# In-projection as Strassen's seven products over quadrants of weights and tokens, in four blocks

## The chip, the cores and the metric

The kernel runs as one program on one core of a Trainium2 chip. The metric is the device time of one execution in microseconds (us). Where this text speaks of the engines it uses the names of the profile: PE (matrix multiply), PEld (its weight loads), DVE (vector), ACT (scalar), POOL (GpSimd) and SP (the queue from which nearly all DMAs of this kernel are issued).

## The reference, cut to what matters

One layer over 2,048 prompt tokens and 8 x 16 sample tokens, model width 1,024, everything in float32:

```
qm, km, vm, om, ip, fp, qa, ka, va = split_in(x @ w_in)   # widths 512 x4, 4, 4, 512, 128, 128
km = km * 128 ** -0.5
logi = ip + b_igate;  logf = log_sigmoid(fp + b_fgate)
hm = sigmoid(om) * head_norm(mlstm_chunkwise(qm, km, vm, logi, logf, state), g)
qa, ka = rope(qa), rope(ka)
ha = swa(qa, ka, va, sinks)                               # window of whole chunks
h = layer_norm(alpha * x + concat(hm, ha) @ w_out)
y = layer_norm(alpha * h + conv_ffn(h))
```

The change is about `x @ w_in`. Of its 2,824 columns 2,560 (qm, km, vm, om, qa) are called the five groups here; the other 264 are the gates and attention's keys and values. The result is wanted to float32 accuracy. The kernel therefore splits each operand into a high and a low part and makes every product in three matmuls (high x high, high x low, low x high).

## The kernel before

**Stages.** The 17 tiles of 128 tokens (16 is the sample tile) are worked through in blocks `BLOCKS = [[16,0,1],[2..5],[6..9],[10..13],[14,15]]`. First comes the in-projection of all five blocks (`i_block`, L379), then the out-projection with the first layer norm over the same blocks (`o_block`, L1049), then the feed-forward part in three larger blocks (`f_ups`, `f_downs`). The two feed-forward projections are already made by seven products over quadrants, the up-projection with two sets of three accumulator banks that alternate (`f_product` L1274, `f_after` L1284).

**In-projection.** Per block the query and key columns come first, feature-major: eight feature tiles, each 8 x 3 matmuls with the weights stationary and all tokens of the block (256 to 512) moving. Then `group` (L355) makes the gates-and-keys columns (264 wide) and three groups of 512 columns token-major: for each tile 8 x 3 matmuls with the tokens stationary and the weights moving. Three accumulator banks (`dps`) go round; each result is copied or rotated out of its bank (L403 to L431) through a ring of three `zev` buffers and stored to DRAM.

**Weights.** `w_split` (L298) loads a unit of 128 x 1024 weights, copies it to the high part on ACT (L194) and subtracts for the low part on DVE (L195); four raw buffers, five high and five low ones. All 24 units of a block are loaded and split again for every block. **Tokens** are loaded and split by `x_slice` (L333), eight slices per block, the low part on DVE or, from the second block on, for odd slices on POOL (L352).

**The weave.** Attention work of finished blocks (the sample chain, the mLSTM chain, the window-attention chain) is cut into steps. `Chains.weave` (L162) advances a clock by the cost that each piece of dense work yields, and puts in a chain step when it is due; a chain may use a block's results once `i_done` is past that block. `until` (L176) forces chain steps before an out-projection block loads their results. The order on PE is the order of the program; it is never changed. Five accumulator banks (`tps`) belong to the chains, so that three are left for dense work. Sums of the down-projection's weights are prepared on the way (`d_sums`, L442).

## Time and profile before

| what | value |
|---|---|
| median of 3 runs | 2448.58 us (2445.84 to 2454.03) |
| the profiled execution | 2448.26 us, its span 2446.3 us |
| granted PE clock, mean | 0.993 |
| in-projection (0 to 777 us) | PE busy 758.34, DVE 459.93, ACT 358.26, POOL 166.89, DMA share 0.63 at 205 GB/s |
| out-projection (777 to 1020 us) | PE busy 232.25, DVE 186.30, ACT 110.77, POOL 86.38, DMA share 0.61 at 209 GB/s |
| chain that ended last | PE 73%, DVE 12%, DMA 5%, issue 4%, ACT 4%, POOL 2% |

Busy time counts an instruction from start to its modelled end. A matmul's duration of 0.28 to 0.41 us in the rows includes the way through the array, which overlaps the next matmul; what a matmul costs in a stream is the distance from its start to the next one's start, which is called its pitch here. The pitch is read from the timeline, not from the mean of a group.

### The profile page before, as it was taken

To read this page: it belongs to the slowest core of one execution; us is meant where nothing else is said; L and a number is where in the kernel's file an instruction comes from. 1 tells how busy PE (TensorE), PEld (TensorE's weight loads), DVE (VectorE), ACT (ScalarE), POOL (GpSimd) and SP (SyncE) were. 2 spreads that over 40 slices of the span, in tenths; PEclk is the share of its full clock that TensorE was granted. 3 is DMA by queue.
4 is the path that set the end of the run, shared out by engine and by line. 5 is a ranking of instruction groups with operands and counts; after the bars stand their busy time and mean duration, and the time that the engine had idled before them with its cause. 6 is when DMAs were issued, how large, how long until landed. Compare 5 with 4: busy or idle time off the path is not lost.

```text
span 2446.3 us, 36879 instructions
## 1 busy us (share of the span) xinstructions
PE 2389.1 (98%) x13004; PEld 2109.5 (86%) x13004; DVE 1760.2 (72%) x3094; ACT 1205.4 (49%) x2235; POOL 398.1 (16%) x444
## 2 busy tenths in 40 slices
PE   9989999999999999999999999999999999999998
PEld 8877878778877778899999999999999978778776
DVE  5566655455477767997788776778766677896897
ACT  4324455355355533655555555445554544444543
POOL 1121322122123333300000000002000100210400
PEclk9999999999999999999999999999999999999999
DMA  8887744544557557588777889987988776656652
GB/s 276 300 302 241 232 134 139 185 126 143 178 185 244 169 208 262 181 300 305 289 267 274 266 307 321 315 283 242 327 293 263 242 275 213 233 181 217 211 189 103
DMA packets 277512, 576.14 MB, mean 236 GB/s; under 512 B 45352, under 2 KB 122156, under 8 KB 277328
## 3 DMA queue, kind: packets, MB, share of 16 engines
q1 hardware_dynamic: 275600, 567.50, 68.6%
q0 software_dynamic: 1728, 6.29, 0.7%
q8 instruction: 103, 1.69, 0.3%
q14 instruction: 81, 0.66, 0.1%
HBM read 419.92 MB, written 153.78 MB: 235 GB/s over the span
## 4 chain that ended last, share of the span: by engine, by line
PE 73%; DVE 12%; DMA 5%; issue 4%; ACT 4%; POOL 2%; SPq 0%; DVEq 0%; POOLq 0%; ACTq 0%
PE dps L1282 15%; PE fup L1282 14%; PE dps L199 8%; PE dps L200 7%; PE dps L201 7%; PE fht L1479 5%; PE dps L1479 5%; PE fup L1479 4%; DMA zf<-cc 2%; DVE cc L1330 2%; DVE wlo L195 2%; DMA ty<-wdn 1%; ACT cc L1328 1%; PE ppo L839 1%; PE ppt L833 1%
## 5 line engine op out<-in xcount | busy, mean ns | idle before, releaser
L1282 PE MATMUL dps<-hh,uw 128*128 128x384 f32 (+1 forms) x1848 | 480.5, 328 | 5.2 <-ACT u L1307 2.9
L1282 PE MATMUL fup<-hh,uw 128*128 128x384 f32 (+1 forms) x1848 | 481.1, 328 | 2.6 <-ACT u L1307 2.4
L195 DVE TENSOR_TENSOR wlo<-wraw,whi 128x1024 fp32r<-128x1024 f32 (+3 forms) x289 | 343.3, 1193 | 158.4 <-ACT whi L194 155.9
L194 ACT CAST whi<-wraw 128x1024 fp32r<-128x1024 f32 (+3 forms) x289 | 282.1, 981 | 288.6 <-PE dps L1479 94.0
L1282 PEld LDWEIGHTS dps<-hh,uw 128*128 128x128 f32 x1848 | 329.8, 188 | 7.0 <-ACT u L1307 4.1
L1282 PEld LDWEIGHTS fup<-hh,uw 128*128 128x128 f32 x1848 | 329.9, 188 | 4.9 <-ACT u L1307 3.9
L1330 DVE SCALAR_TENSOR_TENSOR cc<-u,cw,cc 128x768 f32<-128x768 f32 (+1 forms) x264 | 252.6, 978 | 109.8 <-ACT cc L1328 107.8
L199 PE MATMUL dps<-whi,xh 128*128 128x512 f32 (+1 forms) x816 | 317.7, 389 | 0.0
L200 PE MATMUL dps<-wlo,xh 128*128 128x512 f32 (+1 forms) x816 | 309.6, 379 | 2.8 <-DVE wlo L195 2.8
L201 PE MATMUL dps<-whi,xl 128*128 128x512 f32 (+1 forms) x816 | 309.6, 379 | 0.4 <-POOL xl L352 0.4
L1282 PE MATMUL fup<-hl,uw 128*128 128x384 f32 (+1 forms) x924 | 302.5, 327 | 2.4 <-DVE hl L195 2.4
L1282 PE MATMUL dps<-hl,uw 128*128 128x384 f32 (+1 forms) x924 | 302.3, 327 | 0.0
L199 PEld LDWEIGHTS dps<-whi,xh 128*128 128x128 f32 x816 | 154.9, 190 | 45.5 <-issue 16.5
L1328 ACT ACTIVATE cc<-u,cw 128x768 f32<-128x768 f32 (+1 forms) x132 | 129.6, 998 | 121.0 <-DVE u L1321 59.7
L200 PEld LDWEIGHTS dps<-wlo,xh 128*128 128x128 f32 x816 | 155.0, 190 | 31.9 <-DVE wlo L195 4.0
L201 PEld LDWEIGHTS dps<-whi,xl 128*128 128x128 f32 x816 | 154.6, 189 | 32.1 <-POOL xl L352 0.8
L1282 PEld LDWEIGHTS fup<-hl,uw 128*128 128x128 f32 x924 | 173.5, 188 | 2.8 <-DVE hl L195 2.8
L1282 PEld LDWEIGHTS dps<-hl,uw 128*128 128x128 f32 x924 | 173.5, 188 | 0.0
L1479 PE MATMUL fup<-whi,fu 128*128 128x512 f32 x484 | 158.5, 399 | 7.1 <-DVE yacc L1508 4.5
L1479 PE MATMUL dps<-whi,fu 128*128 128x512 f32 x440 | 149.0, 395 | 0.0
L1479 PE MATMUL fht<-whi,fu 128*128 128x512 f32 x396 | 132.2, 396 | 0.2 <-DVE yacc L1508 0.2
L195 DVE TENSOR_TENSOR uw<-wv,uw 128x512 fp32r<-128x512 f32 x132 | 90.7, 687 | 49.3 <-ACT uw L194 46.8
(285 smaller groups left out, 4343.0 us busy)
## 6 DMA issues: line engine op xcount, KB each, us to landing
uw<-zw SPq DMA_DIRECT2D x176, 512.0 KB, 5.1
zw<-uw SPq DMA_DIRECT2D x88, 512.0 KB, 2.9
wv<-wup SPq DMA_DIRECT2D x66, 512.0 KB, 5.2
wraw<-wtm SPq DMA_DIRECT2D x60, 512.0 KB, 4.7
wraw<-zt SPq DMA_DIRECT2D x60, 512.0 KB, 4.5
wraw<-wdn SPq DMA_DIRECT2D x45, 512.0 KB, 4.8
wraw<-wqk SPq DMA_DIRECT2D x40, 512.0 KB, 4.9
wraw<-wo SPq DMA_DIRECT2D x40, 512.0 KB, 4.7
```

The lines of the kernel that those rows point to most:

```text
L194: nc.scalar.copy(hi, src)
L195: nc.vector.tensor_sub(lo, src, hi.bitcast(F32))
L199: mm(out, ah, bh, start=start, stop=False)
L200: mm(out, ah, bl, start=False, stop=False)
L201: mm(out, al, bh, start=False, stop=stop)
L833: nc.tensor.transpose(pp[:, j * P:(j + 1) * P], scs[kvh][:, j, kt * P:(kt + 1) * P], self.ident)
L839: nc.tensor.matmul(po[64 * kvh:64 * kvh + 64], w, pts[:, kvh], start=kt == 1, stop=kt == nk)
L1282: mm(ps, l[:, k], r[:, k], start=s in (1, 7) and k == 0 and i == 0, stop=k == 3 and i == 2, skip_group_check=True)
L1328: S.activation(c[:, v], u[:, v, 2:2 + n], AF.Identity, bias=w[3], scale=w[2])
L1330: V.scalar_tensor_tensor(c[:, v], u[:, v, i:i + n], w[i], c[:, v], op0=ALU.mult, op1=ALU.add)
L1479: mm(ps, l[:, k, c], r[:, k], start=s in (1, 4, 7) and u == 0 and k == 0 and i == 0, stop=u == nu - 1 and k == n - 1 and i == 2, skip_grou ...
```

## The change

**Products.** The blocks of the in-projection become `IBLOCKS = [[0,1,2,3,16],[4..7],[8..11],[12..15]]`; the out-projection keeps its five (`OBLOCKS`). For each of the five groups of 512 columns and each block of 512 prompt tokens, weights and tokens are cut into quadrants (512 rows of the model width by 256 columns or tokens), and seven products of quadrants or of their sums take the place of eight. A product is 2 x 4 x 3 matmuls with 256 moving columns into one bank (`i_product`). The sample tile is not Strassen's: its four plain products ride on the same weights in block 0, again 256 wide. Gates, keys and values stay direct, 264 wide (`i_direct`).

**Banks.** Three banks A, B, C are held throughout (`ib`). Products 1 and 2 go to A, 6, 5 and 3 to B, 7 and 4 to C; between them ACT copies a bank out or A into B, and DVE adds C to a copy (`i_after`).

**Weight sums.** In block 0 the four quadrants of a group are loaded, and four sums are made in place on DVE and stored to DRAM (`zws`); later blocks load quadrants and sums, seven units per group. **Token sums** are made per block in place in four raw tiles (`x_steps`).

**Buffers.** Four high and four low weight buffers in place of five; weights are loaded up to four units ahead of their split. Token tiles are single, one pair for each product. In the out-projection tokens come in pairs of rows, 1024 wide (`x_pair`), and the running sums `ymix` lie in the token tiles of the in-projection. In the feed-forward part two extra weight buffers (`wx`) make up for the two taken away.

```diff
+IBLOCKS = [[0, 1, 2, 3, 16], [4, 5, 6, 7], [8, 9, 10, 11], [12, 13, 14, 15]]
+OBLOCKS = [[16, 0, 1], [2, 3, 4, 5], [6, 7, 8, 9], [10, 11, 12, 13], [14, 15]]
...
-            for b in range(nb):
-                chains.weave(self.with_sums(b, self.i_block(b)))
-                self.i_done = b + 1
+            chains.weave(self.i_dense())
...
-                if i >= 22 and n < AHEAD:
+                if n < (0, 2, 4, 5)[min(max(i - 22, 0) // 4, 3)]:
                     self.f_next()
...
+    def i_begin(self):
+        self.ib = [self.dps.tile([P, 512], F32, name="dps", tag="dps") for _ in range(3)]
...
+            if b == 0:
+                it += [("p", 0, 0, s) for s in (1, 2, 7, 6)]
+            else:
+                it += [("p", b, 0, s) for s in (1, 7, 6, 2)]
+            for g in range(NG):
+                if g:
+                    it += [("p", b, g, s) for s in (6, 2)]
+                it.append(("p", b, g, 5))
+                if g + 1 < NG:
+                    it += [("p", b, g + 1, 1), ("p", b, g, 4), ("p", b, g, 3), ("p", b, g + 1, 7)]
+                else:
+                    it += [("p", b, g, 3), ("p", b, g, 4)]
+            it += [("t", b, i, b) for i in ((2, 3, 4, 0, 1) if b == 0 else (0, 1))]
+            if b + 1 < nb:
+                it += [("t", b + 1, i, b) for i in (2, 3)]
...
+    def raw_free(self):
+        n = 3 if self.spare else 4
+        return len(self.raws) < n or all(e[1] for e in self.raws[-4:len(self.raws) - n + 1])
+
+    def advance(self):
+        while self.next_split() or self.next_raw():
+            pass
...
+    def split_first(self, g, s, hi, lo):
...
+        if s == 7:
+            V.tensor_sub(r[a11], r[a11], r[a21])
+            keep(a11, 7)
+        elif s == 6:
+            V.tensor_add(r[a21], r[a21], r[a22])
+            keep(a21, 5)
+            V.tensor_sub(r[a11], r[a22], r[a11])
+            keep(a11, 6)
...
+            self.split(hi[:, c], lo[:, c], f[:, c])
+        if s == (6 if g == 0 else 2):
+            V.tensor_sub(r[a12], r[a12], r[a11])
+            keep(a12, 3)
...
+    def i_product(self, b, g, s):
+        mm = self.nc.tensor.matmul
+        ps = self.ib[{1: 0, 2: 0, 6: 1, 5: 1, 3: 1, 7: 2, 4: 2}[s]]
+        wh, wl = self.wu["p", b, g, s]
+        hh, hl = self.hx[b, s]
+        for c in range(2):
+            m = slice(c * P, c * P + P)
+            o = ps[:, c * HT:(c + 1) * HT]
+            for k in range(4):
+                for i, (w, x) in enumerate(((wh, hh), (wh, hl), (wl, hh))):
+                    l, r = (w[:, k, m], x[:, k]) if g < 2 else (x[:, k, m], w[:, k])
+                    mm(o, l, r, start=s in (1, 7) and c == k == i == 0, stop=k == 3 and i == 2, skip_group_check=True)
+                if k % 2:
+                    yield 645
...
+    def i_after(self, b, g, s):
...
+        if s == 1 and g == 0:
+            nc.scalar.copy(B, A)
+        elif s == 6:
+            self.u2 = self.mp.tile([P, 512], F32, name="u2", tag="u2", bufs=1)
+            copy(self.u2, B)
+        elif s == 2:
+            self.i_out(b, g, 0, 0, A)
+        elif s == 5:
+            u4 = self.zev()
+            copy(u4, B)
+            add(u4)
+            self.i_out(b, g, 1, 1, u4)
+        elif s == 4:
+            add(self.u2)
+            self.i_out(b, g, 1, 0, self.u2)
+            if b == 0:
+                self.i_batch(g)
+        elif s == 3:
+            self.i_out(b, g, 0, 1, B)
+            if g + 1 < NG:
+                nc.scalar.copy(B, A)
...
+    def x_pair(self, b, p):
...
+        nc.scalar.copy(h, raw)
+        (nc.gpsimd if b < nb - 1 and p % 2 else nc.vector).tensor_sub(l, raw, h.bitcast(F32))
...
     def f_slot(self, dt=F32R):
-        self.slot = (self.slot + 1) % 2
-        return self.wp.tile([P, KD, P], dt, name="uw", tag=("whi", "wlo")[self.slot], bufs=5)
+        self.slot = (self.slot + 1) % 10
+        if self.slot < 8:
+            return self.wp.tile([P, KD, P], dt, name="uw", tag=("whi", "wlo")[self.slot % 2], bufs=WB)
+        return self.wx.tile([P, KD, P], dt, name="uw", tag="wex", bufs=2)
```

In `i_dense` the items run in this order; after each product its two weight halves are released, `i_after` is emitted, and `advance` emits the next split (for the product four places on) and the next load. `add` is on DVE: C plus the copy (scaled for the key half). `i_out` copies or rotates a finished quadrant into a `zev` buffer and stores it. The token steps run on ACT for the high part and on DVE for the low part, but on POOL for b12 and 4 in block 0 and for 2, 4 and 5 in the other blocks.

## The prediction

> **What bounds the kernel now.** I read the page's engine shares first, then the busy time by stage, then the timelines of PE and DVE.

> ```profile
> span 2446.3 us, 36879 instructions
> PE 2389.1 (98%) x13004; PEld 2109.5 (86%) x13004; DVE 1760.2 (72%) x3094; ACT 1205.4 (49%) x2235; POOL 398.1 (16%) x444
> ```

> By stage (columns: window, length, busy us of PE, PEld, DVE, ACT, POOL with instruction counts, granted clock, DMA share, GB/s):

> ```profile
> 0.00:61.00 61.00, 56.95 (x314) 53.33 (x315) 31.70 (x59) 27.42 (x47) 7.76 (x15) 1.00 0.81 276
> 150.00:777.00 627.00, 615.88 (x3572) 503.93 (x3571) 370.68 (x1160) 302.17 (x795) 139.51 (x142) 0.99 0.58 186
> 777.00:1020.00 243.00, 232.25 (x1087) 183.37 (x1086) 186.30 (x322) 110.77 (x199) 86.38 (x55) 0.97 0.61 209
> 1020.00:1900.00 880.00, 871.40 (x5237) 866.79 (x5236) 675.26 (x900) 480.07 (x815) 72.83 (x156) 1.00 0.83 287
> ```

> The reader is to see that PE is the bound in every stage, with DVE at 59% in the in-projection (370.68 of 627) and 77% behind it (186.30 of 243; 675.26 of 880). So matmul time taken out of the in-projection comes off the end, unless PE begins to wait for DVE or ACT. The pitch of a matmul is read from start to start:

> ```profile
> 676.26 0.28 PE L200 MATMUL dps<-xl,whi 128*128 128x256 f32 x1
> 676.38 0.28 PE L201 MATMUL dps<-xh,wlo 128*128 128x256 f32 x1
> 676.50 0.28 PE L199 MATMUL dps<-xh,whi 128*128 128x256 f32 x1
> 676.62 0.28 PE L200 MATMUL dps<-xl,whi 128*128 128x256 f32 x1
> ...
> 476.92 0.40 PE L200 MATMUL dps<-wlo,xh 128*128 128x512 f32 x1
> 477.15 0.39 PE L201 MATMUL dps<-whi,xl 128*128 128x512 f32 x1
> 477.38 0.40 PE L199 MATMUL dps<-whi,xh 128*128 128x512 f32 x1
> ```

> With 256 columns moving it is 0.12 (median of the last block 0.118), with 512 it is 0.2335, with 384 and 264 0.174 and 0.121. So 256 columns cost half of 512, although each has a weight load of its own; the nearest thing to a floor is the 128-column transposes, 0.11 apart (eight from 203.59 to 204.35). The new shape stands just above it.

> **The matmuls.** Before: queries and keys 192 at 0.174, 576 at 0.2335, 192 at 0.118; three groups 17 x 24 x 3 = 1224 at 0.2335; gates and keys 408 at 0.121: 33.4 + 134.5 + 22.7 + 285.8 + 49.5 = 525.9 us. After: 20 group-blocks x 7 products x 24 = 3360, and 240 for the sample tile, at 0.118 = 424.8; gates and keys unchanged 49.5; eight transposes 0.9: 475.2. **Minus 50.7 us**, all on the bounding engine.

> **What DVE and ACT get.** Rows of the first 777 us:

> ```profile
> L195 DVE TENSOR_TENSOR wlo<-wraw,whi 128x1024 fp32r<-128x1024 f32 x103 | 127.7, 1246 | 64.6 <-ACT whi L194 64.0
> L468 DVE TENSOR_TENSOR zev<-dps,ropet 128x512 f32<-128x512 f32 x17 | 11.6, 684 | 22.2 <-PE dps L201 22.2
> L352 DVE TENSOR_TENSOR xl<-xraw,xh 128x512 fp32r<-128x512 f32 x12 | 10.0, 835 | 3.3 <-ACT xh L351 3.3
> ```

> Splits of weights: 140 against 100 full units, 40 x 1.246 = 49.8, and four gate units fewer at 0.70, -2.8. Low parts of tokens on DVE: 21 x 1.246 = 26.2 against 16.5. Sums of tokens 16 and of weights 20, each 1024 wide at 1.22 (the median of L195): 43.9. Sample tile 4 x 0.69 = 2.8. The 40 additions of C, 512 wide, 40 x 0.69 = 27.6. Together +131: DVE goes from 459.9 of 777 us (59%) to 591 of about 750 (79%). ACT gets 40 splits and the larger token copies at 1.05 us and about 40 copies of 512 at 0.59: 358 + 76 = 434, 58%. DMA: 105 + 20 weight loads and 20 stores of 0.52 MB against 100 loads are +23 MB on 159, about 240 GB/s; the stage behind runs at 287 with PE busy 99%, so bandwidth costs nothing. SP's own queue: a load of weights now waits for the split four units on; as loads lie eight products (23 us) ahead and land in about 5, the cover is 15 us.

> **The start, +10 us (5 to 17).** Now the first product needs one 0.2 MB token slice and a weight unit: it starts at 6.1 us, and the first 61 us lose 8. After, nine transfers of 0.52 MB come first; the first weights land at 4.3, the later ones about 1.9 apart at 276 GB/s: the second token quadrant at 12, the fourth at 18, the last weights at 20. Product 1 can start at 8.5. Product 7 needs, from 18 on, two token sums, a weight sum and two low parts in a row on DVE (6.2 us): it starts at 24, when PE has been free since 19.5. Product 6 has 3.7 us of weight sums and splits and as much for tokens behind that: 31. By 34 PE has done 14 us of work, 20 lost, 10 more than now.

> **The banks, +13 us (0 to 45).** This is the real question. Before, a bank was filled in 5.6 us and two others were free. After, the order is 5, 1', 4, 3, 7', 6', 2': what reads a bank has the length of *one* product, 24 x 0.118 = 2.83 us, plus the chain steps put in (223 us of chain slots beside 526 dense: on average 1.2 more). Five hand-overs per group have this slack: three copies on ACT, the addition after 4 on DVE, and after 5 a copy on ACT and then an addition on DVE before 4 may write C. What they will take I read off the evictions of now, from the last matmul of the bank to the end of its reader. In the three middle blocks the 48 plain ACT copies take 0.93 in the median, 3 of them over 2.83. The 12 rotations (two DVE operations, 1.36 of service) take 1.39, 3 over 2.83. The 12 key tiles, which go ACT, DVE, ACT, take 3.2, 10 over 2.83. Where DVE is fuller (75% from 650 on) the last block's rotation is an example; its matmul was issued at 770.64 and ends at 771.04:

> ```profile
> 771.86 0.68 DVE L468 TENSOR_TENSOR zev<-dps,ropet 128x512 f32<-128x512 f32 x1
> ...
> 775.68 0.42 DVE L813 CUSTOM_DVE_ANT_0 sc<-psc,k_mswa 128x256 f32<-128x256 f32 x1
> ...
> 776.02 0.69 DVE L468 TENSOR_TENSOR zev<-dps,ropet 128x512 f32<-128x512 f32 x1
> 776.70 0.69 DVE L469 TENSOR_TENSOR rb<-dps,ropet 128x512 f32<-128x512 f32 x1
> ```

> A burst of attention on DVE stood in front, and 6.3 us went by. PE would then stand, and behind it the chains' own matmuls in the same queue. Against 4.0 us of slack I charge 0.4 us for the hand-over after 5, 0.2 after 4, 0.1 for each copy, 0.9 per group; 15 groups with chains give 13, block 0's five, without chains, nearly none. Ends: nothing, as the 80% DVE of 870 to 1020 us costs PE 1.5 us; 3 us per group, 45, if responses are like the last block's.

> **Further.** At the three block boundaries the first token pair can be overwritten only after the last direct tile; a copy of 1.05 and a low part of 1.25 then fit in the 5.8 us of two direct tiles, but the chains start at the same moment: +4 (0 to 10). In the out-projection one weight buffer fewer leaves 4.2 us between a unit's release and its next use for 2.3 us of splitting, and POOL's low parts double in width, from 1.59 to an estimated 3.2: +3 (0 to 12). [...] The chains begin later, as block 0 is longer, but by the weave's own costs the last chain tile still ends before the fourth out-projection block, as now, and no forced step arises: 0. The feed-forward start makes five instead of six weights ahead, from four steps later, each on time for products 2.1 us apart: 0 (-2 to 2).

> **Sum.** 2446.3 - 50.7 + 10 + 13 + 4 + 3 = 2425.6 span; 2.0 lie around it; **2428 us**. The profiled execution, 2448.26, is the median of the runs within 0.4, so nothing is added.

> **Rivals.**
> (1) *The slack suffices.* The hand-overs are ordered ahead of the other work and cost nothing, the start 5: 2446.3 - 50.7 + 5 + 3 + 2 = 2406. For it: 45 of 48 ACT copies inside 2.83. Against: DVE at 79%.
> (2) *Given back.* Hand-overs of 2.2 us per group (33) eat the gain: within 0.3% of now.
> (3) *Slower, by the single set of banks.* If the hand-over after 5 waits behind attention's bursts as at 771, 4 us per group, 15 x 4 = 60: 2446.3 - 50.7 + 17 + 60 + 2 = 2475. It decides from 2.7 us per group (41 us) on. For it: the 3.2 us of the ACT-DVE-ACT tiles and the up-projection, which has two sets of banks. Against: with PE standing, DVE catches up, so the wait limits itself.
> (4) *The change doesn't shorten PE.* At a pitch of 0.130 instead of 0.118 for 3600 matmuls, +43: 2471. Against: the rows above.

> **Chances.** Forecast (2410 to 2441) 0.46, (1) 0.18, (2) 0.13, (3) 0.20, (4) 0.03. Under 0.3% (7.3 us) this kernel's measurement tells no change. Faster 0.64, same 0.13, slower 0.23. The range takes in most of (1) and (3): 2402 to 2472; the forecast alone would have 2410 to 2441.

> **What would show it.** Right: the 256-wide matmuls 0.118 apart; PE waits that name copies of a bank on ACT and additions on DVE, some 13 us in all; DVE near 79% before the out-projection; first product after 8 us; feed-forward part unchanged in length. Wrong: waits on those two over 40 us, or waits for weight splits or landings; a dense stretch with a wider pitch; an out-projection or feed-forward part longer by more than 10 us.

## The result, and the profile after

The changed kernel takes 2524.38 us (median of 4 runs, 2520.63 to 2530.84) against 2447.47 us (4 runs, 2445.84 to 2454.03): 1.0312 times as long, interval 1.0282 to 1.0342. The forecast was 2428 us, so its sign was wrong, and its range, which ended at 2472, did not reach the time. The profile below is of the slowest of the four, 2530.84 us, so it shows some 6 us more than the median.

The page of the changed kernel (the span; PE's busy time; the granted PE clock in 40 slices of 63 us):

```profile
span 2529.0 us, 39907 instructions
...
PE 2372.6 (94%) x14425; PEld 2169.9 (86%) x14425; DVE 1899.0 (75%) x3181; ACT 1271.5 (50%) x2282; POOL 425.6 (17%) x431
...
PEclk9989898997998999999999999999999999999999
```

PE is busy for 16 us less than before, 2372.6 against 2389.1, and the span is 83 us longer: PE waits. The slices with a granted clock under 0.9 all lie among the first 14, ahead of the feed-forward part. By stage (columns: window, length, busy us and counts of PE, PEld, DVE, ACT, POOL, granted clock, DMA share, GB/s), the start, the in-projection from 150 us on, the out-projection and the first 880 us of the feed-forward part, which answer to the four rows of before:

```profile
0.00:61.00 61.00, 47.41 (x346) 44.92 (x347) 48.66 (x59) 29.55 (x42) 9.34 (x8) 0.94 0.80 282
150.00:799.00 649.00, 577.02 (x4444) 533.01 (x4443) 463.08 (x1153) 338.58 (x784) 174.98 (x141) 0.93 0.67 210
799.00:1096.00 297.00, 260.99 (x1280) 205.35 (x1280) 213.10 (x451) 129.68 (x254) 98.06 (x61) 0.94 0.58 189
1096.00:1976.00 880.00, 867.27 (x5192) 860.31 (x5191) 672.65 (x894) 476.85 (x807) 67.89 (x153) 1.00 0.83 286
```

The in-projection ends at 799 us instead of 777, the out-projection at 1096 instead of 1019. No engine is full in either: DVE, which the prediction feared, stands at 71% (463.08 of 649). The loss is not spread over the in-projection. The same columns for the passages from block 1 to 2 and from block 2 to 3, and for the stretch behind the second:

```profile
372.00:420.00 48.00, 32.49 (x222) 30.84 (x222) 41.24 (x107) 22.58 (x63) 26.61 (x21) 0.79 0.56 168
575.00:640.00 65.00, 43.02 (x283) 37.98 (x283) 52.98 (x117) 25.41 (x60) 31.38 (x22) 0.77 0.56 181
640.00:800.00 160.00, 155.47 (x1230) 143.16 (x1229) 110.00 (x279) 98.64 (x222) 35.49 (x28) 0.98 0.69 212
```

Inside a block PE is busy for 97% (155.47 of 160) at a clock of 0.98. At a passage it is busy for two thirds of the time, at a clock of 0.77 to 0.79, and DVE is at 82 to 86%. What PE waited for up to the end of the out-projection (line waited at, releaser, us in total, times, longest):

```profile
PE pgr L947 <- DVE g L938: 30.2, 3, 11.7
PE dps L657 <- ACT zev L668: 16.5, 3, 6.5
PE pq L1155 <- DMA qa<-zqa: 9.5, 1, 9.5
PE pcol L965 <- DVE ql L204: 8.4, 2, 8.3
PE dps L631 <- ACT zev L707: 5.9, 2, 4.8
```

L631 is the product, the place for which 13 us of waits were predicted; L657 is the direct tile (gates, keys, values). `pgr` is the first PE instruction of the mLSTM chain in a block, `pq` that of the window-attention chain, `pcol` one of the mLSTM chain's rows. These waits lie at passages or right behind the last block, all but 1.1 us of the last row. In the profile before, the longest rows of this view, up to 1020 us, were:

```profile
PE ppt L833 <- POOL sc L823: 3.7, 2, 2.1
PE ppt L986 <- POOL scs L980: 3.3, 1, 3.3
```

**The account.** For each matmul the time from the end of the one before it to its own end is set against the pitch of its shape; what is over is a wait, or, where the granted clock is half, the stretch of the matmul itself. Up to the end of the out-projection, in us:

| | before | after |
|---|---|---|
| dense matmuls | 718.5 | 666.9 |
| attention's matmuls | 232.9 | 234.6 |
| waits | 58.2 | 157.4 |
| stretch by the half clock | 9.9 | 36.8 |
| (time at half clock, waits included) | 27.3 | 139.9 |
| end of the out-projection | 1019.4 | 1095.5 |

So 51.6 us of matmuls were saved, waits took 99 and the half clock 27 more: +76. The feed-forward part adds 7 (1434 against 1427).

**One passage from close by.** PE between the last direct tile of block 2 and the first of block 3 (start, length, the instruction, and in brackets the wait ahead of it and its releaser):

```profile
604.98 0.42 PE L657 MATMUL dps<-w,ol 128*128 128x264 f32 x1
617.13 0.37 PE L947 MATMUL pgr<-ident,g 128*4 128x128 f32 x1 [11.73 <-DVE g L938]
...
622.09 0.64 PE L657 MATMUL dps<-w,oh 128*128 128x264 f32 x2
622.53 0.42 PE L657 MATMUL dps<-w,ol 128*128 128x264 f32 x1
...
630.78 0.40 PE L657 MATMUL dps<-w,oh 128*128 128x264 f32 x2
631.03 0.28 PE L657 MATMUL dps<-w,ol 128*128 128x264 f32 x1
```

DVE in that time:

```profile
605.93 0.29 DVE L803 TENSOR_TENSOR rb<-dps,ropet 128x128 f32<-128x128 f32 x1
608.23 3.35 DVE L489 TENSOR_TENSOR xr<-xr 128x1024 f32<-128x1024 f32 x1 [2.01 <-POOL ol L511]
611.50 1.34 DVE L511 TENSOR_TENSOR ol<-xr,oh 128x1024 fp32r<-128x1024 f32 x1
612.76 0.30 DVE L922 TENSOR_TENSOR g<-gates,k_gb 128x32 f32<-128x32 f32 x1
...
616.81 0.17 DVE L938 SCALAR_TENSOR_TENSOR g<-gl,g 128x16 f32<-128x16 f32 x1
```

and POOL:

```profile
605.86 4.63 POOL L511 TENSOR_TENSOR ol<-xr,oh 128x1024 fp32r<-128x1024 f32 x2
```

The gates of block 2 leave the last direct tile at 605. Before their logarithms can begin on DVE (L922 to L938, 4.2 us of small operations, first to last) stand two token steps of block 3, one of which took 3.35 us (608.23 to 611.58), where its like take 1.22 (L489, median), while POOL's second low part ran to 610.49. Only at 617 can PE make `pgr`; everything behind it on PE waits, although the next direct tile needs nothing of it. And behind the wait a pair of the tile's matmuls takes 0.44 us (622.09 to 622.53), at half clock, where later it takes 0.25 (630.78 to 631.03). Before the change the gates were made in the first token-major group, some 67 us ahead of the block's end (three groups of 96 matmuls at 0.2335), and `pgr` waited for 0.3 us in all. Not every passage loses in this way: from block 1 to 2 the mLSTM chain is still at block 0, and PE stands for 8.3 us because a split of attention's own on DVE (`ql`, 380.16) is queued behind token sums, weight splits and evictions.

### The profile page after: what moved, and what is told of

The parts are those of the page before. It is cut to its first block, busy times and chain, and to the rows that moved or that the text cites. A ratio compares the mean times of both kernels' runs of the same rounds, so it can differ in the third digit from the quotient of the medians.

```text
span 2529.0 us, 39907 instructions
## 1 busy us (share of the span) xinstructions
PE 2372.6 (94%) x14425; PEld 2169.9 (86%) x14425; DVE 1899.0 (75%) x3181; ACT 1271.5 (50%) x2282; POOL 425.6 (17%) x431
## 4 chain that ended last, share of the span: by engine, by line
PE 54%; DVE 11%; issue 4%; DMA 3%; ACT 3%; POOL 2%; SPq 0%; DVEq 0%; POOLq 0%; ACTq 0%
PE dps L1676 15%; PE fup L1676 14%; PE fht L1879 5%; PE dps L1879 5%; PE dps L631 3%; PE fup L1879 3%; DMA zf<-cc 2%; PE dps L208 2%; PE dps L209 2%; PE dps L210 2%; DVE cc L1724 1%; DVE uw L204 1%; DVE w L204 1%; ACT cc L1722 1%; PE ppo L1228 1%
## 5 line engine op out<-in xcount | busy, mean ns | idle before, releaser
L204 DVE TENSOR_TENSOR w<-wraw,w 128x1024 fp32r<-128x1024 f32 (+2 forms) x199 | 258.6, 1307 | 100.7 <-ACT w L203 93.7
L203 ACT CAST w<-wraw 128x1024 fp32r<-128x1024 f32 (+2 forms) x199 | 198.4, 1003 | 218.2 <-PE dps L631 91.7
L631 PE MATMUL dps<-w,oh 128*128 128x256 f32 x1344 | 263.8, 290 | 16.3 <-ACT zev L707 5.9
L631 PEld LDWEIGHTS dps<-w,oh 128*128 128x128 f32 x1344 | 218.1, 194 | 30.8 <-issue 9.7
L204 DVE TENSOR_TENSOR uw<-wraw,uw 128x1024 fp32r<-128x1024 f32 x126 | 150.8, 1199 | 61.2 <-ACT uw L203 61.0
L631 PE MATMUL dps<-w,ol 128*128 128x256 f32 x672 | 192.0, 286 | 0.0
L631 PE MATMUL dps<-oh,w 128*128 128x256 f32 x896 | 177.5, 291 | 14.1 <-DVE zev L711 5.0
L1879 PE MATMUL fup<-uw,fu 128*128 128x512 f32 x726 | 176.1, 398 | 9.0 <-DVE yacc L1908 4.6
L631 PEld LDWEIGHTS dps<-oh,w 128*128 128x128 f32 x896 | 146.2, 196 | 23.7 <-issue 6.6
L1879 PE MATMUL dps<-uw,fu 128*128 128x512 f32 x660 | 164.4, 395 | 0.0
```

The costliest lines, as they stand in the source:

```text
L203: nc.scalar.copy(hi, src)
L204: nc.vector.tensor_sub(lo, src, hi.bitcast(F32))
L631: mm(o, l, r, start=s in (1, 7) and c == k == i == 0, stop=k == 3 and i == 2, skip_group_check=True)
L1879: mm(ps, l[:, k, c], r[:, k], start=s in (1, 4, 7) and u == 0 and k == 0 and i == 0, stop=u == nu - 1 and k == n - 1 and i == 2, skip_grou ...
```

## The experiments

Theory A, formed from these views: PE waits at the passages, because the gates and keys of a block are now its last results and attention's first PE instructions are placed right behind them. Where an expectation says A2, it is A widened after the first runs: not the gates alone, but the whole burst that meets at a passage on DVE, ACT and POOL, the next block's token steps included. "After" below is the changed kernel, 2524.4 us. The ratio is that to the kernel before, run beside it on the same chip; the kernel before took 2447.5 to 2451.6 us (medians) in these series, so a difference of a few us to "after" is no difference.

### The logarithms of the gates early

```diff
             while self.i_done <= b:
                 yield 0, 500
+            if b not in self.glog:
+                self.logs_of(b)
+                yield 0, 14000
...
```

and the same two steps in `t_sample` ahead of its `gate_rows`: DVE is given the logarithms, and the chain's PE instructions come 14 us of the weave's clock later.

> The gate logarithms of a block are put out as soon as its last direct tile is emitted, and the first chain step that needs them comes 14 us (by the weave's costs) later; nothing else changes. Theory A (the loss sits at the block boundaries: PE stands at the transposes of the gates, 7.2 + 12.0 + 11.8 us, and runs at half clock behind them): 31 us of waits go and some 10 to 20 us of half-clock stretch with them, 2475 to 2490. Theory B (the single set of banks and a full DVE are the bound, the waits only move to the next hand-over): 0 to 12 us, 2512 to 2524.

Measured: 2502.16 us, 1.0215 (1.0189 to 1.0240), 22 us less than after, between the two expectations. PE's waits from 150 us to the out-projection's end:

```profile
PE pq L1158 <- DMA qa<-zqa: 20.1, 1, 20.1
PE dps L657 <- ACT zev L668: 10.5, 4, 4.5
PE dps L631 <- ACT gates L664: 9.3, 1, 9.3
```

No `pgr` waits for logarithms any more: the wait is where A has it. But one wait of 20.1 us for a load of window-attention takes up part of the gain, at the end of the last block, where the changed kernel has 9.5. The chain behind the one that was put off became the first to arrive too early.

### A second buffer for the rotated keys

```diff
-        B = self.mp.tile([P, 512], F32, name="rb", tag="rb", bufs=1)
+        B = self.mp.tile([P, 512], F32, name="rb", tag="rb" if ti % 2 else "u2", bufs=1)
```

> The rotation of the keys in the direct tiles takes its second product in the buffer u2, free at that time, for every other tile, in place of the one buffer that the rotation of the last group still holds. Theory A (at the boundary a direct tile waits for the copy out of its bank, 6.4 + 7.0 + 4.5 us, because the rotations queue up for one buffer behind POOL): 8 to 20 us less, 2504 to 2516. Theory B: no change, within 4 us of 2524.

Measured: 2522.80 us, 1.0301 (1.0280 to 1.0321), 2 us less than after: no change, as theory B has it. The keys' single buffer is not what the direct tiles wait for.

### Logarithms, loads and buffer together

The two edits above, and window-attention's loads issued 14 us ahead of their transposes (`swa_load` in two halves):

```diff
-        kv, pq, pk = self.swa_load(t)
+        new = self.swa_fetch(t)
+        if self.place(t)[1] == 0:
+            yield 0, 14000
+        kv, pq, pk = self.swa_turn(*new)
...
```

> e1 and e2 together, and in the window attention the loads of a block's first tile are issued 14 us ahead of its transposes. Theory A: boundary waits of 31 + 18 + 9.5 us and most of the half-clock stretch go, 2435 to 2460. Theory B: 2505 to 2520.

Measured: 2505.50 us, 1.0232 (1.0210 to 1.0255). This misses theory A and lies at the edge of theory B's range: no better than the logarithms alone. The 20 us wait went, and waits of 4 to 8 us came in the direct tiles of the passages instead. That a chain no longer stands in front does not help as long as the direct tiles themselves wait for the same engines.

### Matmuls put into the gap

56 matmuls of the identity with itself into a bank of the chains, ahead of each block's first chain instruction, to hold the clock up:

```diff
             if pend is None:
+                if b not in self.glog:
+                    self.fill()
                 pend = self.m_rows(t, b, ti)
...
```

> Ahead of the first gate transposes of each block PE makes 56 matmuls of the identity with itself (about 7.3 us, four times, 29 us of needless work; the output doesn't use them) while it would wait for the gate logarithms. If the drop to half clock behind a wait costs time of its own, PE stays at full clock there and the time falls by 5 to 15 us although work is added. If the clock plays no part, the needless work hides in the wait: within 4 us of 2524. If the waits are not where the profile puts them, 29 us are added: 2553.

Measured: 2538.45 us, 1.0367 (1.0344 to 1.0391), 14 us more than after, which none of the three expectations has. The trace shows the added matmuls at three places (from 173, 612 and 807 us), as 336 records, two for each matmul, which take some 40 us: 13 at each place, where 7.3 were expected. In the account above, waits fall by 31 us, and the stretch by the half clock stays (37.5 against 36.8), although the time at half clock in the in-projection behind 150 us falls from 96 to 82 us. So the added work fills waits; that it saves anything by the clock is not shown.

### The tokens of blocks 1 to 3 left out

```diff
     def x_steps(self, b, *steps):
+        if b:
+            for s in steps:
...
+                    self.hx[b, s] = self.hx[0, s]
...
+            return
```

Loads, sums and splits of these blocks' tokens go; block 0's stand in for them.

> Blocks 1 to 3 use block 0's token tiles: their token loads, sums, copies and low parts are left out (per block about 11 us of DVE, 8 of ACT, 7 of POOL and 2 MB, all at the block boundary), so the output is that of wrong tokens. Theory A2 (at a boundary ACT, DVE and POOL get more work than PE's dense work there can cover, and PE stands until they are through, whichever dependency is the last): the direct tiles' waits and part of the waits for gate logarithms go, 25 to 50 us less, 2475 to 2500. Rival (the order of the dependencies alone: logarithms on PE's path; e1 moved some): under 10 us less, 2514 or more.

Measured: 2491.50 us, 1.0158 (1.0138 to 1.0178), 33 us less than after, as A2 has it. The waits for `pgr` shrink from 30.2 to 21.2 us and those of the direct tiles for `zev` from 16.5 to 4.5: the next block's tokens are in front of the gates, but are not all of it.

### The low parts of blocks 1 to 3 on DVE

```diff
-(nc.gpsimd if s in ((2, 4, 5) if b else ("b12", 4)) else V).tensor_sub(
+(V if b else nc.gpsimd if s in ("b12", 4) else V).tensor_sub(
```

> The three low parts of tokens per block that POOL makes (2.34 us each) go to DVE (1.23 us each). If POOL's operations hold up DVE's at the boundary (a token sum of 1.22 us took 3.35 beside one of them), 4 to 12 us less, 2512 to 2520. If DVE's load counts, 4 to 10 us more.

Measured: 2515.81 us, 1.0256 (1.0236 to 1.0277), 9 us less than after, although DVE, the fuller engine, has nine operations of 1.22 us more. The runs of the two just touch (2511.29 to 2520.66 against 2520.63 to 2530.84); the same edit on the spread-out version below is clearer. The sum L489 on DVE (min/median/max in ns), first in the changed kernel:

```profile
L489 DVE TENSOR_TENSOR xr<-xr x3: 1216/1225/3345, 169.2 to 608.2; 128x1024 f32<-128x1024 f32 x3
```

and with the low parts on DVE:

```profile
L489 DVE TENSOR_TENSOR xr<-xr x3: 1212/1212/1219, 165.7 to 602.7; 128x1024 f32<-128x1024 f32 x3
```

The stretched one, which began at 608.23 and ended at 611.58, about one operation's length behind POOL's end at 610.49, is gone. How much of the 9 us is that, and how much that one operation takes POOL 2.3 us (4.63 for two) and DVE 1.2, these runs do not separate.

### The direct tiles in the middle of the block

For blocks 1 to 3 the two last direct tiles go into the third group, behind its products 1 and 7, and into a bank of the chains; the logarithms follow them; loads early as above.

```diff
             for g in range(NG):
+                if b and g == 2:
+                    it += [("t", b, i, 10 + b) for i in (0, 1)]
                 if g:
                     it += [("p", b, g, s) for s in (6, 2)]
...
```

> In blocks 1 to 3 the two direct tiles of the block's first tokens move from its end to its middle (into a bank of the chains), the gate logarithms follow them there, and the first loads of window attention are issued 14 us ahead of their transposes; the boundary keeps two direct tiles and the token steps. Theory A2: boundary work is spread, waits of 45 to 65 us go and 15 us of half-clock stretch, 2445 to 2470. Rival (the waits move on to the banks' hand-overs inside the groups): 2495 to 2510, as e1.

Measured: 2508.58 us, 1.0233 (1.0217 to 1.0249), 16 us less than after, in the rival's range. PE's waits from 150 us on:

```profile
PE dps L209 <- DVE w L204: 10.7, 5, 3.2
PE dps L663 <- DVE ol L513: 9.7, 2, 5.3
PE dps L637 <- ACT zev L674: 9.1, 2, 7.1
```

The waits of L209 are the out-projection's, for low parts of weights. L663 is now the direct tiles of the *next* block, which came right behind the last product and need a pair of token tiles that had just been asked for (`ol`, L513). The gates were helped, the tokens were next in line.

### Early logarithms and loads, without the tokens

The first experiment with the early loads and with the tokens of blocks 1 to 3 left out as above.

> e1 (logarithms early), the early loads of window attention, and e6 (blocks 1 to 3 use block 0's tokens, their token work is left out) in one. Theory A2 (dependencies at the boundary and the burst of token work there are two parts of the loss that add up): 22 + 33 and some 10 for the load, 2455 to 2470. Rival (each only uncovers the same wait of ACT and DVE behind it): 2485 to 2495, no better than e6.

Measured: 2464.56 us, 1.0068 (1.0052 to 1.0085), 60 us less than after, as A2 expected: 22 for the logarithms and 33 for the tokens make 55 of it. No wait over 4.2 us is left behind 150 us:

```profile
PE dps L639 <- ACT dps L743: 8.5, 3, 4.2
PE dps L209 <- DVE w L204: 7.5, 5, 2.4
PE dps L665 <- ACT zev L676: 6.5, 4, 3.5
```

Even so it is not faster than before.

### The passages spread out

All of the computation, with the direct tiles placed apart: two in the middle of the block, two behind the products 1 and 7 of the block's first group; the token steps shared out to match; loads and the sample's logarithms early. The second version has the low parts of blocks 1 to 3 on DVE as well.

```diff
-                it += [("p", b, 0, s) for s in (1, 7, 6, 2)]
+                it += [("p", b, 0, s) for s in (1, 7)]
+                it += [("t", b, i, 20 + b) for i in (2, 3)]
+                it += [("p", b, 0, s) for s in (6, 2)]
...
-        passage = {7: ["load"], 5: [7], 3: [3], 4: ["b12", "t1", "t2"]}
+        passage = {7: ["load"], 2: [1], 5: [7], 3: [3], 4: ["b12", "t1", "t2"]}
...
```

> A whole computation again: as e8, and the next block's direct tiles of its second half come after its first two products, the token parts are spread over products around the boundary, the sample's logarithms come 14 us ahead. Theory A2: boundary waits fall by 45 to 60 us in all and the half-clock stretch by 15, 2450 to 2475. Rival: waits move into the groups, 2495 to 2510.

> e10 with the low parts of tokens that POOL makes given to DVE. As in e7, about 9 us less than e10 if POOL's operations hold up DVE's; 0 to 10 us more if DVE's load decides.

Measured: 2491.79 us, 1.0172 (1.0157 to 1.0188), between the two expectations; with the low parts on DVE 2478.71 us, 1.0119 (1.0104 to 1.0134), 13 us less again. That is the best version that leaves nothing out: 46 us less than after, 30 more than before. Its longest waits:

```profile
PE dps L209 <- DVE w L204: 12.5, 5, 6.8
PE dps L638 <- ACT zev L714: 9.5, 3, 7.0
PE dps L638 <- DVE ol L513: 6.2, 4, 2.0
PE dps L664 <- ACT zev L675: 5.7, 1, 5.7
```

They name different producers at different places, and no single one of them stands out.

### Waits put into the kernel before

Does a wait cost more than its length? In the kernel before, after two (or six) of the eight feature tiles of each block, PE is made to wait for a short chain ACT, POOL, PE:

```diff
             nc.sync.dma_start(self.zqk[b][ft], ev[:, :W])
+            if ft in (4, 6):
+                self.pause(6)
...
+    def pause(self, n):
...
+        nc.tensor.transpose(ps[:, 0], self.ident, self.ident)
+        nc.scalar.copy(w, ps[:, 0])
+        for _ in range(n):
+            nc.gpsimd.tensor_mul(w, w, w)
+        nc.tensor.transpose(ps[:, 1], w, self.ident)
```

The second kernel has `if ft in (2, 3, 4, 5, 6, 7)` and `self.pause(1)`.

> The kernel before, with ten waits of PE put into its in-projection (behind feature tiles 4 and 6 of each block): a transpose, its copy on ACT, six small operations on POOL, and a transpose of the result, some 4 to 5 us each; the output doesn't use them. If a wait of this length makes PE run at half clock afterwards, the time rises by the waits (40 to 50 us) and 15 to 30 us of half-clock stretch, and half-clock time rises by 35 to 70 us. Rival (the clock costs nothing): by the waits alone.

> The kernel before, with thirty short waits (behind feature tiles 2 to 7 of each block, one operation on POOL each), some 1.5 us each, 45 us in all. If only waits beyond a length bring the half clock, the time rises by the waits (35 to 50 us) with under 5 us of stretch; if every wait does, by 20 us more.

Measured, ten long waits: 2521.94 us, 1.0285 (1.0247 to 1.0322). What PE waited for, and its clock up to the out-projection's end:

```profile
PE ppause L496 <- POOL pause L495: 41.1, 10, 5.3
```

```profile
0.00:1099.00 1099.00, 1027.11 (x5382) 838.41 (x5383) 650.01 (x1635) 471.74 (x1093) 283.78 (x285) 0.95 0.57 191
```

The out-projection ends 80 us later (1099.0 against 1019.2), for ten gaps of 44 us in all. By the account, 31 of the other 36 are stretch, as the time at half clock goes from 27 to 113 us; 2 are the twenty added transposes and 3 other waits. The four runs took 2512.45 to 2530.73 us, 63 to 81 more than the kernel before, at mean clocks of 0.983 to 0.975; the profile is of one of 2527.76. So the clock's part varies from run to run. The time at half clock rose by 85 us in the profile, more than the 35 to 70 expected. One of the gaps:

```profile
382.63 0.47 PE L496 MATMUL ppause<-ident,pause 128*128 128x128 f32 x1 [5.29 <-POOL pause L495]
...
383.32 0.63 PE L200 MATMUL dps<-xl,whi 128*128 128x512 f32 x1
383.75 0.63 PE L201 MATMUL dps<-xh,wlo 128*128 128x512 f32 x1
...
387.47 0.40 PE L201 MATMUL dps<-xh,wlo 128*128 128x512 f32 x1
387.70 0.40 PE L199 MATMUL dps<-xh,whi 128*128 128x512 f32 x1
```

After the wait the matmuls are 0.43 apart until 387.3, then 0.23 again. Measured, thirty short waits: 2539.00 us, 1.0365 (1.0349 to 1.0381): some 70 us of waits more than before, where 45 were planned: mostly 0.9 to 2.5 us each, with a few of 4 to 8. The time at half clock is 68 us instead of 27, the added stretch 11 us, and the sixty transposes take some 7. So a wait of about 4 us cost its length and 0.7 of it again in that profile (31 on 44), the shorter ones 0.16 again (11 on 70); in the changed kernel it was 0.27 (27 on 99). Neither branch of the second expectation, under 5 or 20 us of stretch, was met.

## Why the prediction was wrong

The same account for six versions, up to the end of the out-projection, in us:

| | waits | time at half clock | median of the runs |
|---|---|---|---|
| before | 58 | 27 | 2447.5 |
| after | 157 | 140 | 2524.4 |
| tokens left out | 126 | 92 | 2491.5 |
| spread out | 127 | 92 | 2491.8 |
| spread out, low parts on DVE | 112 | 92 | 2478.7 |
| logarithms and loads early, tokens left out | 102 | 68 | 2464.6 |

- **Matmuls, -50.7: right.** The products are 0.118 apart, as in block 2:

```profile
550.02 0.28 PE L631 MATMUL dps<-w,ol 128*128 128x256 f32 x1
550.14 0.40 PE L631 MATMUL dps<-w,oh 128*128 128x256 f32 x2
550.38 0.28 PE L631 MATMUL dps<-w,ol 128*128 128x256 f32 x1
```

  Dense time fell by 54.2 us in the in-projection, and rose by 2.6 in the out-projection. Rival 4 falls.
- **The start, +10: right.** 19.3 us lost in the first 61 instead of 8.2: +11, though the first product began at 6.4 us and not at 8.5.
- **The banks, +13 (0 to 45): right in size.** Waits over 0.7 us inside the groups that name copies of a bank on ACT or additions on DVE come to some 19 us, and 24 with the one of 4.8 us that lies at a passage and is counted there. Rival 3, which had the slower time, put it here and falls with its mechanism: DVE is at 71% and not 79%, mainly as the stage is longer (570.5 us busy up to 799, against 591 predicted).
- **The block boundaries, +4 (0 to 10): the step that failed.** Nine waits of 4.5 to 12.0 us at three passages and at the end of the last block add up to 72.5 us. The prediction looked only at the next block's first token pair, and gave 4 us for the remark that "the chains start at the same moment", without working it out. Three things meet there: the evictions of the direct tiles, the next block's token steps, and the logarithms of the gates. In the kernel before, the direct tiles were made three groups ahead of the block's end, and the logarithms needed only them.
- **Chains later, 0: failed with it.** "The chains begin later" was read as a question of when the last one ends. What mattered was what their first PE instruction waits for: the gates had moved from the first token-major group to the last tiles, which the working did not follow up.
- **The clock: not in the sum at all.** 27 us of stretch behind the waits, with no term and no end of the range for it.
- **Out-projection, +3 (0 to 12): mis-sized by what was left out.** It is 54 us longer in time; 22 of that are attention's matmuls that the in-projection no longer holds (20 less there), 27 waits. Of the waits 21.7 are the last block's passage (11.8 for `pgr`, 9.9 for `pq`).
- **Feed-forward, 0 (-2 to 2): slightly off**, +7, in small waits spread over it (33.5 against 26.8 us); not followed further.

The experiments show the passages as the cause by the logarithms (-22), the tokens (-33) and both with the loads (-60). The two with the tokens take work away and don't only move it; the version in which DVE takes over POOL's low parts is faster, which speaks against DVE's mere load as the cause. The rest, from 2464.6 to the forecast, is the waits that were left, 44 us more than before, and their half clock. That a placement exists which keeps the 51 us was not shown; the best whole version is 1.2% slower than before.

## What to carry to other kernels

When a result is made later in its stage, find its first reader on the engine that bounds the kernel and works in the order of the program (here the 11.73 us at `pgr`, with a direct tile behind it that needed nothing of it), and price the whole way from the result to that reader, with everything that is queued in front of it on the engines between; a mean share of 71% on such an engine says nothing about a place where three bursts meet. When matmuls are saved on an engine that was 98% busy, the waits between them have to be kept short too, as each cost 1.2 to 1.7 times its length here, by the clock. Removing one wait of a cluster shows the next: the logarithms early, the loads early and the tiles in mid-block each uncovered another, and only taking logarithms, loads and tokens out of the passages together gave the sum.
